# Hybrid decoder layer on one core: sines computed earlier, the picks' transposes placed behind their chunks, new pacing of the gathered rows, low parts in strict turn, a fourth set of split tiles

## The chip, the cores and the metric

The kernel runs on one core of one Trainium2 chip. The metric is the device time of one execution in microseconds (us); of several executions the median is taken. Engines are named as the profile names them: PE (TensorE matmuls), PEld (its weight loads), DVE (VectorE), ACT (ScalarE), POOL (GpSimd) and SP (SyncE, which here issues most of the DMAs).

## The reference

One layer on 512 tokens of width 2048, all in float32:

```python
z = rmsnorm(x) @ w_in                       # columns: pool | q | k | v
x = x + concat(pool_mixer(z), dilated_attention(rope(q), rope(k), v)) @ w_out
x = x + cross_attention(rmsnorm(x), rmsnorm(mem))      # 4 heads, 256 memory tokens
h = rmsnorm(x)
q = (h @ w_pq).reshape(T, 8, 2, 128)
s1, s2 = q[:, :, 0] @ sub_keys_1.T, q[:, :, 1] @ sub_keys_2.T
# per token and head: top 16 of s1 and of s2, their 256 sums, the top 16 of those
gates = softmax(sc); experts = e1 * 128 + e2          # 128 of 16384 experts a token
c = gates * gelu(sum(h * w_u[experts]))
x = x + sum(c * w_v[experts])
out = rmsnorm(x)
```

`rope` turns the first 32 of each head's 128 channels by angles `positions * inv`; it needs sines and cosines of these.

## The kernel before, in words

Every matmul of a weight is split in three, since PE works on rounded operands: a weight tile of 128 x 1024 is loaded by SP (`wraw`), ACT writes its rounded high part `wh` (L143), and DVE or POOL writes the low part `wl = wraw - wh` (L144); `mm3` (L149 to 152) then multiplies `wh` by the high and the low part of the activations, and `wl` by the high part. The pool `wp` holds three pairs `wh`, `wl` and four `wraw`, so the splitting can run about three tiles ahead of PE. A "chunk" is one output block of 128 columns: two such tiles, 48 matmuls (`proj_one`). `lo_eng` says which engine writes the low parts: one for both halves, or a pair for the first and second half.

The 512 tokens are treated in two parts. The first 128 go through the whole attention part alone, in a row layout (0 to 380 us, with `w_pq_f` as the last weight, four groups, 318 to 378 us). Their experts are then evaluated by gathering: for each of 128 picks, POOL issues an indirect DMA that fetches 128 rows of `w_u` (1 MB, L114), DVE takes the dot product with the token (`dot0`, L318); after a gelu the same rows of `w_v` are added up on DVE (`axpy0`, L331). This `queue` of DVE work is threaded between the chunks of everything else: `behind(n)` adds `n` to a debt and issues an entry for each whole unit. The tuple `RATE` sets `n` per chunk by stage: the heads' chunks of `z`, the pool chunks, `w_out`, the cross-attention scores, the scores and picks of `w_pq`, and the gates.

The other 384 tokens follow in the transposed layout: the heads (380 to about 730 us), `w_out` (to 880), cross attention with `w_co` as its last weight (to 991), the scores `w_pq` (to 1137). 64 of them are gathered as well (`dot1`, `axpy1`, their token rows kept in `hy1`); the last 320 go through all 16384 experts densely. The dense part has 128 chunks of `w_u` (`a_chunk`): the first 21 run beside the three `pick`s (7 each, 1137 to 1290), in which DVE finds the top 16 sums of 128 tokens each; 35 more run beside the 80 `gates` (1353 to 1676), in which DVE builds one-hot tiles `u` (L1114, L1116) from the transposed picks and PE multiplies them (L1119). From 1676 us on (`c_chunk`) chunks 56 to 127 are computed and used at once: a group of 8 chunks is multiplied by 16 tiles of `w_v` (the loop over `dd`, PE's L150 to L152 into `pa`), while the next group's 8 chunks of `w_u` are computed (into `pm`). This lasts to 2663 us; the 56 chunks computed before then only need `w_v` (to 3152).

What sets the order: the code's order is handed to a scheduler that works with its own timeline, and it may lay instructions of one engine in another order than the code has; SP and, from the dense part on, POOL keep the code's order. Each engine then runs its list strictly in order. So where a transpose waits for DVE, all matmuls listed behind it wait too.

Three places matter below. In the attention's beginning (L754 to 767) `cosT` and `sinT` are computed from the positions (DVE, with two sines on ACT), and `rope` (L771 to 776) multiplies by them on POOL. In the loop over the picks (L1038 to 1061) PE transposes the pick's result (L1054 to 1056) when DVE has it (`e12`, L1052):

```python
pick(b) ... TE.transpose(pt, e12, ident) x3 ; copies to e12T, gT
a_until(KB * b + KB)      # the 7 chunks of w_u that run beside pick b
```

And in `a_chunk` (L1021 to 1027) the low parts of chunks 64 and up are on POOL for even chunks (both halves) and on DVE for odd ones, while the loop over `dd` has DVE and POOL in turn for `w_v`.

## Time and profile before

| | us |
|---|---|
| median of 3 runs | 3184.94 (3177.57 to 3185.37) |
| the profiled execution's own time | 3175.37 |
| its span | 3173.6 |
| PE busy | 2947.7 (93%) |
| DVE busy | 2422.7 (76%) |
| POOL busy | 1433.8 (45%) |
| ACT busy | 1298.6 (41%) |
| bytes moved | 912.79 MB, mean 288 GB/s |

The busy times are sums over the span; an engine that waits for another is not busy. Since PE leaves 226 us of the span unused, the waits in front of its instructions, stage by stage, are what is to be read. "PEclk" is the granted clock as a share of the full one: a stage with PEclk below 1 has had stretches at half speed, and its busy time is longer by them.

### The profile page before, as it was taken

Reading aid. Unit: us, or ns where it says so; the run is one execution under the profiler, and the core shown is the slowest. Engines: PE = TensorE matmul, PEld = TensorE weight load, DVE = VectorE, ACT = ScalarE, POOL = GpSimd, SP = SyncE. Lnnn points to the kernel's source line nnn. Section 1 sums busy time; section 2 is a strip of 40 time slices with the busy share of each in tenths; the row PEclk is TensorE's granted clock in tenths of the full one; section 3 lists DMA queues with packets and bytes.
Section 4 is the critical chain, followed back from the end, with each engine's and each line's share of the span. In section 5 each row is a group of like instructions: output and inputs, shape, how many; then the busy total and the mean of one; then the engine's idle time right before and its main releaser. Section 6 shows DMA issues by size and latency. Waiting matters only on the chain.

```text
span 3173.6 us, 47405 instructions
## 1 busy us (share of the span) xinstructions
PE 2947.7 (93%) x18311; PEld 2832.5 (89%) x18311; DVE 2422.7 (76%) x3360; ACT 1298.6 (41%) x1789; POOL 1433.8 (45%) x826
## 2 busy tenths in 40 slices
...
GB/s 261 295 300 214 244 119 282 330 309 339 342 266 192 111 127 124 182 302 318 315 304 315 357 325 359 357 367 355 330 372 353 353 354 358 346 357 362 343 163 106
DMA packets 243521, 912.79 MB, mean 288 GB/s; under 512 B 23488, under 2 KB 85600, under 8 KB 192224
## 3 DMA queue, kind: packets, MB, share of 16 engines
...
q8 instruction: 144, 2.36, 0.3%
q14 instruction: 81, 0.66, 0.1%
...
## 4 chain that ended last, share of the span: by engine, by line
PE 66%; DVE 20%; DMA 5%; issue 5%; ACT 2%; POOL 0%; ACTq 0%; POOLq 0%; DVEq 0%; SPq 0%
PE pm L150 11%; PE pm L152 11%; PE pm L151 11%; PE pa L152 9%; PE pa L150 9%; PE pa L151 9%; DVE wl L144 2%; DVE u L1114 2%; DVE oh L295 1%; DVE oh L293 1%; PE pm L400 1%; PE pm L401 1%; PE pm L399 1%; PE pa L1119 1%; DMA rows<-in_w_v_rows_dram,sidx 1%
## 5 line engine op out<-in xcount | busy, mean ns | idle before, releaser
L144 POOL TENSOR_TENSOR wl<-wraw,wh 128x1024 fp32r<-128x1024 f32 x369 | 930.5, 2526 | 1433.3 <-ACT wh L143 1401.4
L143 ACT ACTIVATE wh<-wraw 128x1024 fp32r<-128x1024 f32 (+1 forms) x658 | 693.7, 1058 | 1042.1 <-PE pm L151 467.0
L152 PE MATMUL pa<-ch,wl 128*128 128x320 f32 x2048 | 634.5, 312 | 25.4 <-DVE wl L144 23.5
L150 PE MATMUL pm<-dH,wh 128*128 128x320 f32 x2048 | 640.4, 313 | 15.0 <-DVE cl L1164 6.5
L152 PE MATMUL pm<-dH,wl 128*128 128x320 f32 x2048 | 640.6, 313 | 6.1 <-DVE wl L144 3.9
L150 PE MATMUL pa<-ch,wh 128*128 128x320 f32 x2048 | 636.7, 311 | 7.3 <-DVE xT L1193 4.7
L151 PE MATMUL pm<-dL,wh 128*128 128x320 f32 x2048 | 639.0, 312 | 0.0
L151 PE MATMUL pa<-cl,wh 128*128 128x320 f32 x2048 | 635.3, 310 | 0.0
L144 DVE TENSOR_TENSOR wl<-wraw,wh 128x1024 fp32r<-128x1024 f32 (+1 forms) x289 | 377.4, 1308 | 166.5 <-ACT wh L143 158.7
L152 PEld LDWEIGHTS pa<-ch,wl 128*128 128x128 f32 x2048 | 387.1, 189 | 30.4 <-DVE wl L144 28.1
L150 PEld LDWEIGHTS pm<-dH,wh 128*128 128x128 f32 x2048 | 389.2, 190 | 16.3 <-DVE cl L1164 6.8
L150 PEld LDWEIGHTS pa<-ch,wh 128*128 128x128 f32 x2048 | 388.3, 190 | 10.2 <-ACT ch L1163 5.2
L152 PEld LDWEIGHTS pm<-dH,wl 128*128 128x128 f32 x2048 | 389.3, 190 | 8.2 <-DVE wl L144 5.4
L151 PEld LDWEIGHTS pm<-dL,wh 128*128 128x128 f32 x2048 | 389.3, 190 | 0.0
L151 PEld LDWEIGHTS pa<-cl,wh 128*128 128x128 f32 x2048 | 388.1, 190 | 0.0
L150 PE MATMUL pm<-hH,wh 128*128 128x384 f32 x1024 | 355.9, 348 | 10.4 <-DVE k L811 3.4
L152 PE MATMUL pm<-hH,wl 128*128 128x384 f32 x1024 | 354.2, 347 | 10.5 <-DVE wl L144 10.5
L151 PE MATMUL pm<-hL,wh 128*128 128x384 f32 x1024 | 354.4, 346 | 5.2 <-DVE hL L874 4.4
L1193 DVE TENSOR_TENSOR xT<-pa,xT 128x320 f32<-128x320 f32 x256 | 124.7, 487 | 196.6 <-PE pa L152 191.0
L150 PEld LDWEIGHTS pm<-hH,wh 128*128 128x128 f32 x1024 | 197.6, 193 | 17.1 <-issue 5.8
L152 PEld LDWEIGHTS pm<-hH,wl 128*128 128x128 f32 x1024 | 197.6, 193 | 13.4 <-DVE wl L144 12.5
L151 PEld LDWEIGHTS pm<-hL,wh 128*128 128x128 f32 x1024 | 197.7, 193 | 6.9 <-DVE hL L874 4.7
...
## 6 DMA issues: line engine op xcount, KB each, us to landing
wraw<-in_w_u_dram SPq DMA_DIRECT2D x256, 512.0 KB
wraw<-in_w_v_dram SPq DMA_DIRECT2D x256, 512.0 KB
...
```

The costliest lines, as they stand in the source:

```text
L143: S.activation(wh[:, c], raw[:, c], AF.Copy)
L144: i = (lo_eng or V).tensor_tensor(wl[:, c], raw[:, c], wh.bitcast(F32)[:, c], op=ALU.subtract)
L150: TE.matmul(ps, wh, xh, start=start, stop=False)
L151: TE.matmul(ps, wh, xl, start=False, stop=False)
L152: TE.matmul(ps, wl, xh, start=False, stop=stop)
L293: V.tensor_tensor(oh, iota50.unsqueeze(1).broadcast_to([P, 16, NCAND]), cf[:, h, :].unsqueeze(2).broadcast_to([P, 16, NCAND]), op=ALU.is_e ...
L295: V.tensor_tensor(oh, oh, ecand[:, h, :].unsqueeze(1).broadcast_to([P, 16, NCAND]), op=ALU.mult)
L399: TE.matmul(ps, xh, wh, start=start, stop=False)
L400: TE.matmul(ps, xh, wl, start=False, stop=False)
L401: TE.matmul(ps, xl, wh, start=False, stop=stop)
L1114: V.tensor_tensor(u, iota.unsqueeze(1).unsqueeze(1).broadcast_to([P, 2, 4, P]), e12T[:, :, t:t + 4].unsqueeze(3).broadcast_to([P, 2, 4, P] ...
L1193: V.tensor_tensor(xT[:, dd, NS:], ps[:, :ND], xT[:, dd, NS:], op=ALU.add)
```

## The change

1. **Early sines.** The rope tables are computed in hooks of `w_pq_f`'s third group (`pos_in`, `trig_rows`) instead of at the beginning of the attention; `cosT` lives in the pool `kt`, `sinT` in the first 32 partitions of `accx`.
2. **Picks.** `a_until` stands ahead of the transposes, and the transposes are tied behind the last matmul issued (`issue_after(last_mm)`).
3. **RATE.** (3.0, 2.2, 2.5, 2.0, .25, 1.2) becomes (3.2, 2.4, 2.8, 2.5, .25, .95).
4. **Strict turn.** From chunk 64 on the first half's low part of every `w_u` tile pair is on POOL, the second half's on DVE.
5. **A fourth set of split tiles.** `split_tiles`: once `extra[0]` is set (behind the scores), each fourth load takes its pair `whx`, `wlx` from a new pool `wx`.
6. **Gathered tokens in DRAM.** The 64 tokens' rows are written to `hyd` by ACT's DMA queue in four pieces and loaded by `start1`; `end1` uses a row tile. The pool `hy` is gone.
7. **The sums of squares** in the stage of `w_co` (L961 before) add on POOL instead of DVE.

```diff
-RATE = (3.0, 2.2, 2.5, 2.0, 0.25, 1.2)
+RATE = (3.2, 2.4, 2.8, 2.5, 0.25, 0.95)
...
+    sinT = accx[:32]
...
+    def split_tiles():
+        extra[1] += extra[0]
+        if extra[1] % 4 == 3:
+            return wx.tile([P, 1024], F32R, name="whx"), wx.tile([P, 1024], F32R, name="wlx")
+        return wp.tile([P, 1024], F32R, name="wh"), wp.tile([P, 1024], F32R, name="wl")
...
-        wh = wp.tile([P, 1024], F32R, name="wh")
-        wl = wp.tile([P, 1024], F32R, name="wl")
+        wh, wl = split_tiles()
...
-        TE.matmul(ps, wl, xh, start=False, stop=stop)
+        last_mm[0] = TE.matmul(ps, wl, xh, start=False, stop=stop)
...
-            V.tensor_tensor(acc, acc, q, op=ALU.add)
+            (eng or V).tensor_tensor(acc, acc, q, op=ALU.add)
...
+        def pos_in():
+            posr.append(ep.tile([P, TR], F32, name="jk", bufs=2)[:32].bitcast(I32))
+            nc.scalar.dma_start(posr[0], a["positions"][:, T0:].broadcast_to([32, TR]))
+            nc.scalar.dma_start(invf, a["invfreq"])
+
+        def trig_rows():
+            V.tensor_copy(cosT, posr[0])
+            V.tensor_scalar(cosT, cosT, scalar1=invf, scalar2=None, op0=ALU.mult)
+            trig(cosT, ep.tile([P, TR], F32, name="jk", bufs=2)[:32], sinT, cosT)
+            V.tensor_scalar(sinT[0:16], sinT[0:16], scalar1=-1.0, scalar2=None, op0=ALU.mult)
+
+        hooks_x[2][0] = [pos_in]
+        hooks_x[2][5] = [trig_rows]
...
-        nc.scalar.dma_start(posi, a["positions"][:, T0:].broadcast_to([32, TR]))
-        ang = tmp2k()[:32]
-        V.tensor_copy(ang, posi)
-        V.tensor_scalar(ang, ang, scalar1=invf, scalar2=None, op0=ALU.mult)
-        trig(ang, tmp2k()[:32], sinT, cosT)
...
-                sumsq(xtmp, accx, xT[:, c, :], c == 0, TR)
+                sumsq(xtmp, accx, xT[:, c, :], c == 0, TR, eng=G)
...
-        lo = G if j < RB * KB else (V, G) if j < K1 else G if j < K1 + GRP or j % 2 == 0 else V
+        lo = G if j < RB * KB else (V, G) if j < K1 else G if j < K1 + GRP else (G, V)
...
+            a_until(KB * b + KB)
             pt = pa.tile([P, 512], F32, name="pa")
-            TE.transpose(pt[:, 0:P], e12[:, 0, :], ident)
-            TE.transpose(pt[:, P:2 * P], e12[:, 1, :], ident)
-            TE.transpose(pt[:, 2 * P:3 * P], gtf, ident)
+            with tc.issue_after(last_mm[0].ins):
+                TE.transpose(pt[:, 0:P], e12[:, 0, :], ident)
+                TE.transpose(pt[:, P:2 * P], e12[:, 1, :], ident)
+                TE.transpose(pt[:, 2 * P:3 * P], gtf, ident)
...
-            a_until(KB * b + KB)
...
-        S.copy(gx[0], hy1)
+        r = row_tile()
+        nc.sync.dma_start(r, hyd)
+        S.copy(gx[0], r)
...
-        y1[0] = hy.tile([P, D], F32, name="htok")
+        y1[0] = row_tile()
...
-            S.copy(hy1[:, k4 * 512:(k4 + 1) * 512], pt)
+            hs4 = gw.tile([P, 512], F32, name="hs4")
+            S.copy(hs4, pt)
+            nc.scalar.dma_start(hyd[:, k4 * 512:(k4 + 1) * 512], hs4)
```

How this moves instructions is seen in the engines' lists. Line numbers in a list of the changed kernel are its own: its `rope` is L790 to 792, its transposes of a pick L1073 to 1075, its low part L153, its `mm3` L161 to 163, its dot products of the second queue L1095.

POOL, the beginning of its list up to the first head's rope, before (`t2k` is the shuffled copy of `q` or `k`):

```order
L144 TENSOR_TENSOR wl_3339<-wraw_3337,wh_3338 128x1024
L144 TENSOR_TENSOR wl_3441<-wraw_3439,wh_3440 128x1024
L144 TENSOR_TENSOR wl_3579<-wraw_3577,wh_3578 128x1024
L774 TENSOR_TENSOR t2k_3224<-t2k_3224,sinT_3203 32x384
L774 TENSOR_TENSOR t2k_3239<-t2k_3239,sinT_3203 32x384
L775 TENSOR_TENSOR q_3222<-q_3222,cosT_3202 32x384
L775 TENSOR_TENSOR k_3235<-k_3235,cosT_3202 32x384
L776 TENSOR_TENSOR q_3222<-q_3222,t2k_3224 32x384
L776 TENSOR_TENSOR k_3235<-k_3235,t2k_3239 32x384
```

and now:

```order
L153 TENSOR_TENSOR wl_3337<-wraw_3335,wh_3336 128x1024
L153 TENSOR_TENSOR wl_3439<-wraw_3437,wh_3438 128x1024
L790 TENSOR_TENSOR t2k_3222<-t2k_3222,accx_93 32x384
L791 TENSOR_TENSOR q_3220<-q_3220,cosT_116 32x384
L790 TENSOR_TENSOR t2k_3237<-t2k_3237,accx_93 32x384
L791 TENSOR_TENSOR k_3235<-k_3235,cosT_116 32x384
L792 TENSOR_TENSOR q_3220<-q_3220,t2k_3222 32x384
L792 TENSOR_TENSOR k_3235<-k_3235,t2k_3237 32x384
```

Two low parts stand ahead of the rope instead of three, and the sine (`accx`) and cosine tiles come from the stage before.

PE, the second pick's transposes, before:

```order
L152 MATMUL pm_10381<-dH_7905,wl_10414 128x320
L150 MATMUL pm_10445<-dH_7905,wh_10447 128x320
L151 MATMUL pm_10445<-dL_7906,wh_10447 128x320
L1054 MATMUL pa_10117<-ident_86,e12_10111 128x128
L1055 MATMUL pa_10117<-ident_86,e12_10111 128x128
L1056 MATMUL pa_10117<-ident_86,gt_10103 128x128
L152 MATMUL pm_10445<-dH_7905,wl_10448 128x320
```

and now:

```order
L162 MATMUL pm_10531<-dL_7933,wh_10563 128x320
L163 MATMUL pm_10531<-dH_7932,wl_10564 128x320
L1073 MATMUL pa_10595<-ident_86,e12_10136 128x128
L1074 MATMUL pa_10595<-ident_86,e12_10136 128x128
L1075 MATMUL pa_10595<-ident_86,gt_10128 128x128
L161 MATMUL pm_10707<-dH_7932,wh_10709 128x320
L162 MATMUL pm_10707<-dL_7933,wh_10709 128x320
```

They stood in the middle of a chunk and now stand behind one. Counted from the first matmul of `dH`, pick 0's come behind 387 of them (379 before), pick 1's behind 641 (547), pick 2's behind 977 (730); the first gate's matmul behind 1221 (1134).

DVE, a piece of the stage with `w_u` and `w_v`, before (L1075 is a dot product, L1159 and L1164 make `ch`, `cl` of a chunk, L1193 adds a `w_v` product):

```order
L1075 ISA rows,sact_7900<-rows,gx 128x2048
L1075 ISA sact_7900 128x1
L144 TENSOR_TENSOR wl<-wraw,wh 128x1024
L1075 ISA rows,sact_7900<-rows,gx 128x2048
L1075 ISA sact_7900 128x1
L144 TENSOR_TENSOR wl<-wraw,wh 128x1024
L1159 TENSOR_TENSOR pm<-pm,gt 128x320
L1193 TENSOR_TENSOR xT<-pa,xT 128x320
L144 TENSOR_TENSOR wl<-wraw,wh 128x1024
```

and now:

```order
L153 TENSOR_TENSOR wlx<-wraw,whx 128x1024
L1095 ISA rows,sact_7927<-rows,gx 128x2048
L1095 ISA sact_7927 128x1
L153 TENSOR_TENSOR wl<-wraw,wh 128x1024
L1181 TENSOR_TENSOR pm<-pm,gt 128x320
L1186 TENSOR_TENSOR cl<-pm,ch 128x320
L153 TENSOR_TENSOR wlx<-wraw,whx 128x1024
```

Before, DVE's low parts belonged to loads that followed one another (the run over the engines was DVE, three times POOL, three times DVE, POOL); now each is every second load, and each second of these goes to the fourth set.

## Rows read from the trace of the kernel before

**Rows 1.** The page's head: the span, and section 1's busy times

```profile
span 3173.6 us, 47405 instructions
PE 2947.7 (93%) x18311; PEld 2832.5 (89%) x18311; DVE 2422.7 (76%) x3360; ACT 1298.6 (41%) x1789; POOL 1433.8 (45%) x826
```

**Rows 2.** Windows: stretch, length, busy of the engines (instructions), PEclk, DMA share, GB/s

```profile
318.00:378.00 60.00, 50.72 (x232) 38.10 (x231) 51.62 (x127) 34.76 (x39) 1.30 (x1) 0.99 0.79 263
398.00:428.00 30.00, 11.20 (x36) 9.02 (x35) 29.97 (x119) 7.14 (x14) 6.12 (x6) 0.60 0.12 36
480.00:960.00 480.00, 444.77 (x2378) 420.17 (x2377) 385.82 (x478) 184.57 (x319) 244.09 (x171) 0.96 0.83 310
1137.00:1290.00 153.00, 121.52 (x775) 119.03 (x774) 147.92 (x377) 50.63 (x65) 88.56 (x34) 0.89 0.42 130
1353.00:1676.00 323.00, 304.45 (x2166) 299.91 (x2165) 304.08 (x249) 161.31 (x177) 154.80 (x70) 0.98 0.84 307
1741.00:2663.00 922.00, 912.81 (x6184) 910.97 (x6183) 666.39 (x634) 327.38 (x398) 493.83 (x298) 0.99 0.92 352
2663.00:3040.00 377.00, 350.97 (x2311) 344.41 (x2310) 296.21 (x306) 122.36 (x148) 182.64 (x107) 0.98 0.92 343
```

**Rows 3.** Timeline of PE at the attention's start: start, length, line, [idle before <-releaser]

```profile
411.68 1.22 PE L818 MATMUL pa<-kT,q 128*128 128x128 f32 x4 [13.33 <-POOL q L776]
...
416.34 0.80 PE L818 MATMUL pa<-kT,q 128*128 128x128 f32 x2 [2.06 <-DVE t2k L822]
...
421.82 0.66 PE L150 MATMUL pm<-hH,wh 128*128 128x384 f32 x1 [3.40 <-DVE k L811]
```

**Rows 4.** Timeline of PE: the picks' transposes

```profile
1212.44 0.48 PE L1054 MATMUL pa<-ident,e 128*128 128x128 f32 x1 [1.80 <-DVE e L1052]
...
1252.09 0.47 PE L1054 MATMUL pa<-ident,e 128*128 128x128 f32 x1 [10.96 <-DVE e L1052]
...
1289.66 0.45 PE L1054 MATMUL pa<-ident,e 128*128 128x128 f32 x1 [8.03 <-DVE e L1052]
```

**Rows 5.** PE's waits: in 1290:1741 (first row), 1741:2663 (two), 2663:3040 (last)

```profile
PE pa L1119 <- DVE u L1116: 14.7, 11, 3.6
...
PE pa L152 <- DVE wl L144: 6.7, 3, 3.0
PE pm L152 <- DVE wl L144: 2.5, 4, 0.7
...
PE pa L152 <- DVE wl L144: 16.8, 14, 2.3
```

**Rows 6.** Timelines of ACT, DVE and POOL before the attention's start

```profile
395.10 1.28 ACT L236 ACT_TABLE_LOAD   x1
401.23 0.52 ACT L236 ACTIVATE sinT<-t2k 32x384 f32<-32x384 f32 x1 [4.85 <-DVE t2k L235]
...
386.00 0.55 DVE L811 TENSOR_TENSOR k<-ma,r2c 128x384 f32<-128x384 f32 x1
...
386.82 2.39 POOL L144 TENSOR_TENSOR wl<-wraw,wh 128x1024 fp32r<-128x1024 f32 x1 [7.77 <-ACT wh L143]
...
403.88 2.28 POOL L774 TENSOR_TENSOR t2k<-t2k,sinT 32x384 f32<-32x384 f32 x2 [6.34 <-DVE sinT L767]
408.74 0.98 POOL L775 TENSOR_TENSOR q<-q,cosT 32x384 f32<-32x384 f32 x1 [2.57 <-DVE cosT L239]
```

**Rows 7.** Groups by line: DVE over the span; in 940:991; POOL over the span

```profile
L318 DVE CUSTOM_DVE_ANT_0 rows<-rows,gx 128x2048 f32<-128x2048 f32 x66 | 150.0, 2276 | 6.4 <-DMA rows<-in_w_u_rows_dram,sidx 6.4
...
L217 DVE SCALAR_TENSOR_TENSOR hL<-xT,gains,hH 128x384 fp32r<-128x384 f32 x16 | 19.4, 1219 | 4.1 <-ACT hH L216 4.1
...
L225 DVE TENSOR_TENSOR accx<-accx,xtmp 128x384 f32<-128x384 f32 x15 | 8.2, 546 | 0.0
...
L1219 POOL TENSOR_TENSOR xT<-xT,rf 128x384 f32<-128x384 f32 x5 | 6.4, 1315 | 15.1 <-ACT rf L210 15.1
```

**Rows 8.** Timelines of DVE and POOL near 2800 us

```profile
2796.93 0.48 DVE L1159 TENSOR_TENSOR pm<-ga,gt 128x320 f32<-128x320 f32 x1
...
2799.56 2.23 DVE L1159 TENSOR_TENSOR pm<-ga,gt 128x320 f32<-128x320 f32 x1
...
2799.04 2.39 POOL L144 TENSOR_TENSOR wl<-wraw,wh 128x1024 fp32r<-128x1024 f32 x1 [4.79 <-ACT wh L143]
```

More of the change, by code (lines that the diff above doesn't have):

```diff
@@ L94, in hybrid_kernel @@
     rz = const.tile([P, NB], F32, name="rz")[:, :RB]
+    invf = const.tile([32, 1], F32, name="invf")
     accx = const.tile([P, TR], F32, name="accx")
+    sinT = accx[:32]
     xT = big.tile([P, KD, TR], F32, name="xT")
@@ L133, in hybrid_kernel @@
     anchor = [None]
+    extra = [False, 0]
+    def split_tiles():
[3 more added lines that the diff above has]
+        return wp.tile([P, 1024], F32R, name="wh"), wp.tile([P, 1024], F32R, name="wl")
     def load_w(src, lo_eng=None, parts=1):
         raw = wp.tile([P, 1024], F32, name="wraw", bufs=WRAW)
-        wh = wp.tile([P, 1024], F32R, name="wh")
-        wl = wp.tile([P, 1024], F32R, name="wl")
+        wh, wl = split_tiles()
         n = 1024 // parts
@@ L147, in load_w @@
         return wh, wl
+    last_mm = [None]
     def mm3(ps, wh, wl, xh, xl, start, stop):
@@ L365, in hybrid_kernel @@
     halo = kt.tile([P, 8, 16], F32, name="halo")
+    cosT = kt.tile([32, TR], F32, name="cosT")
     def alloc_ma():
@@ L711, in hybrid_kernel @@
             hooks_x[k // 8][k % 8] = [lambda k=k: xr_sq(k)]
+        posr = []
+        def pos_in():
[9 more added lines that the diff above has]
+        hooks_x[2][5] = [trig_rows]
         for g in range(4):
```

11 lines of the change are left out of this document (3 added, 8 removed).

## The prediction

> **What bounds the kernel now.** First the page's head [rows 1]: PE is busy for 2947.7 of 3173.6 us. What can be won without changing PE's work is the other 226 us, and what PE loses to a lower clock while it is busy. No other engine is near the span as a whole (DVE 76%), but a mean hides stages, so the second view is a table of windows, one per stage [rows 2]. There the reader sees three kinds of stage. In 1741 to 2663 PE is busy for 912.81 of 922 us at a granted clock of 0.99, so 9.2 us are all that waits can give. In 2663 to 3040 it is busy for 350.97 of 377, while DMA is at 0.92. And from 1137 to 1290 and from 1353 to 1676 DVE is busy for 147.92 of 153 and for 304.08 of 323 us: there DVE is about as much the bound as PE. The third view is the timeline and the waits, which say what PE stood for. At the attention's start it waits 13.33 us for POOL's rope, then 2.06 and 3.40 us [rows 3]; at the picks' transposes 1.80, 10.96 and 8.03 us [rows 4]; in the gates 14.7 us for the one-hot tiles, and in the dense part for late low parts on DVE [rows 5].
>
> One figure for the pace: 6184 matmuls of 128 x 320 took 912.81 us in 1741 to 2663, 0.1476 us each [rows 2].
>
> **The change, part by part.**
>
> *Early sines: -12 us.* The 13.33 us end with the last rope instruction on POOL. Going back [rows 6]: POOL began at 403.88, after the sine on ACT (401.23), which waited 4.85 us for the angles on DVE; then POOL waited another 2.57 us for the cosine. With the tables there, what is left is `k` (386.00, done at 386.55), two shuffles on DVE, POOL's low part until 389.21 (one of the three is now behind the rope) and the rope: two products in 2.28 us and four instructions of 0.98, together 6.2. That ends at 395.4, 3 us before PE's last chunk (411.68 - 13.33 = 398.35). So the 13.33 go; the next to wait for are the scores' masks and the next chunk on DVE, the 2.06 and 3.40 us that stand there now, in a stretch where DVE is busy for 29.97 of 30 us. I let them grow by 1.3. Ends: -6 if POOL's list is held up by its low parts, -17 if the clock (0.60 in 398 to 428, [rows 2]) recovers as well.
>
> *The price of it: +2.* Two extra loads of ACT's tables, 1.28 us each [rows 6], and eleven DVE instructions go into the first part, whose last stage has DVE busy for 51.62 of 60 us; in the list only three of the eleven fall there, the others in the stage of `w_cq`. The positions' DMA is issued long before. Ends 0 and +4.
>
> *RATE: +4 before the scores, -5 in the gates.* A dot product takes 2.276 us of DVE [rows 7]. By the stages' chunk counts the heads take 2.2 more, the pool chunks 1.6, `w_out` 4.8, the cross scores 2: 10.6, or 24 us of DVE and 11 MB, between 480 and 960, where DVE has 94 us free, and DMA at 0.83 has 82 [rows 2]. In the gates 35 x 0.25 = 8.75 fewer, -20 us of DVE in 323, where PE waits 14.7 us for `u`. Of that I count a third, since DVE remains at 284 of 304 needed by PE. Ends 0 and +15 before, -12 and +10 in the gates.
>
> *Sums of squares on POOL: -3.* Fifteen additions of 0.546 us leave DVE, 8.2 us of a 51-us stage. Nearest price on POOL: 1.315 for a product of the same shape, 20 us in all [rows 7]. What speaks against it: DVE's instruction with two inputs in SBUF runs long beside POOL: 2.23 us beside a low part that POOL began at 2799.04, against 0.48 alone [rows 8]; the `hL` of this stage average 1.219 us. More POOL work makes more such meetings; at 20 more us of it, eight instructions of DVE held for half an addition each are 5 us. The Trainium skill ("SBUF — State Buffer", Who interferes with whom) says the same: a DVE instruction with two inputs in SBUF contends with a GpSimd instruction that reads SBUF, and the later one blocks until the other is done. By that rule alone this edit would give back its 8 us; the trace's 2.23 against 0.48 agrees with it. Ends -6 and +5.
>
> *Picks: -27.* PE's list says what is moved: pick 1's transposes 94 matmuls later, pick 2's 247. At 0.1476 that is 13.9 and 36.5 us, against waits of 10.96 and 8.03 [rows 4]. DVE's picks take as long as now (147.92 of 153). PE came to pick 1's at 1252.09 - 10.96 = 1241.1; it will come at 1255, 3 us behind DVE. To pick 2's it came at 1281.6, of which 11 are then gone: 1270.6 + 36.5 = 1307, 17 behind DVE. So both waits go, and 1 of pick 0's 1.80: 20. The clock's dips that follow such waits go too: 775 matmuls at 0.1476 are 114.4 against the 121.52 shown, 7 us. What is late next: the gates. Their first matmul now comes 87 matmuls (12.8 us) later in PE's list, which leaves DVE nearly as much time as before. Ends -32, and -12 if pick 1's stays.
>
> *Strict turn and a fourth set: -8 in 1741 to 2663, -10 in 2663 to 3040.* In the first stretch PE waits 6.7 + 2.5 us for low parts [rows 5]; with the splitting one load further ahead (24 matmuls, 3.5 us) a low part that is 3.0 late at most comes in time. No more than these 9.2 and a little clock is there. In the second PE loses 26 us, 16.8 of them for DVE's low parts, 14 times, at most 2.3. By the same measure all would go, but DMA is busy for 0.92 of 377 = 347 us there: no less time than PE's own 351. I take 10, ends 0 and -25; for the first stretch +5 and -17.
>
> *Tokens in DRAM: 0.* Four copies and DMAs of 256 KB on ACT and one load of 1 MB on SP, among a thousand loads; its cover is the four `wraw` tiles loaded ahead (14 us). Without that cover it costs the 3 us of one MB at 350 GB/s.
>
> Sum: -12 + 2 + 4 - 5 - 3 - 27 - 8 - 10 = -59, against the profiled execution's 3175.37: 3116. That execution is 9.6 us under the median of the runs and 2 below their lowest, so a median of runs should be some us higher; I add 5: **3121 us**.
>
> **The rivals.**
>
> 1. *DMA holds the dense part.* Then strict turn and the fourth set give nothing: 3121 + 18 = **3139 us**. For it: 0.92 busy at 352 and 343 GB/s [rows 2]. Against it: low parts, not loads, are what PE waited for [rows 5]. The Trainium skill ("SBUF — State Buffer", Summary) gives about 358 GB/s as the limit for traffic between HBM and SBUF; the trace's means lie within 5% of it.
>
> 2. *The earlier dots cost their time.* The 24 us of DVE in 480 to 960 come on PE's path instead of 4: **3141 us**. For it: DVE is busy for 386 of 480 us, in bursts around the picks and softmaxes. Against: 94 us are free.
>
> 3. *The moves don't move the waits.* DVE reaches pick 1 and 2 later, or the rope still waits (for POOL's low parts), so that sines and picks give nothing: 3121 + 39 = **3160 us**. For it: 3 us of margin at pick 1. Against: 17 at pick 2.
>
> 4. *Slower: the strict turn lays POOL's low part beside each of DVE's.* DVE's, with two inputs in SBUF, is then held for the rest of POOL's 2.4 us, and comes late as often as it is held. Its price is that of the late ones today, 16.8 / 14 = 1.2 us, and as much again where the clock falls behind it: 2.4. From (59 - 18 + 10) / 2.4 = 21 late ones on the kernel is slower; with 35 of the 120 DVE low parts in the first stretch late it takes 3139 + 84 = **3223 us**. For it: 2.23 against 0.48 [rows 8]. Against: POOL's share of the loads is the same half as before, and DVE has 256 us free there.
>
> **How the numbers follow.** Forecast 0.50; rivals 1 to 4: 0.16, 0.10, 0.07, 0.07; 0.10 for the gains' upper ends, about 3090. A measurement can tell 0.3% from no change, 9.6 us: faster is below 3175.4, slower above 3194.5. Rival 4 is slower, half of rival 3's bounds reach no change, and some of the others' upper ends do: 0.86, 0.07, 0.07. The sum of all lower ends is 3066 and of all upper ones 3196; neither comes at once. The range 3086 to 3166 holds the forecast and rivals 1 to 3, and leaves out rival 4 and what lies under 3086.
>
> **What would show it.** Early sines: the wait of 13.33 for `q` L776 is gone, those behind it stay under 8 us. Picks: no transpose waits over 2 us, PEclk in that stage 0.95 or more. RATE: DVE about 410 of 480 us in 480 to 960, PE's waits for `u` under 12. Dense part: waits for `wl` under 3 us in the first stretch, under 8 in the second, with PE busy for over 0.95 of it. Wrong would be: new waits in front of the gates as large as those removed; more waits for `wl`; a transfer or POOL as the releaser in 480 to 990.

## The result, and the profile after

The change makes the kernel slower. Four runs of each, side by side: 3211.67 us (3209.63 to 3220.22) against 3181.26 us (3176.87 to 3185.37) before; the ratio of the two means is 1.0101, 95% interval 1.0075 to 1.0127. The prediction said 3121, in a range of 3086 to 3166.

The page of the changed kernel, its head:

```profile
span 3207.8 us, 47207 instructions
PE 2949.9 (92%) x18311; PEld 2829.1 (88%) x18311; DVE 2467.5 (77%) x3345; ACT 1289.1 (40%) x1790; POOL 1501.6 (47%) x841
```

Beside [rows 1]: PE has the same 18311 matmuls and 2.2 us more of busy time, so the other 32 of the 34 us by which the span is longer are waits; DVE is busy for 45 us more although it lost 15 additions. The windows, with stretches that hold about the same work as those of [rows 2]:

```profile
398.00:428.00 30.00, 21.66 (x110) 19.51 (x109) 30.00 (x111) 11.66 (x20) 11.76 (x5) 0.83 0.21 58
480.00:960.00 480.00, 427.00 (x2309) 401.34 (x2308) 400.03 (x485) 179.97 (x307) 256.42 (x182) 0.96 0.86 329
1145.00:1300.00 155.00, 131.27 (x836) 129.97 (x835) 148.83 (x375) 54.61 (x71) 101.99 (x37) 0.91 0.45 135
1737.00:2672.00 935.00, 912.46 (x6118) 905.25 (x6117) 700.36 (x619) 313.42 (x390) 502.16 (x289) 0.99 0.90 340
2677.00:3065.00 388.00, 348.71 (x2298) 341.70 (x2297) 308.96 (x306) 117.89 (x144) 191.28 (x109) 0.97 0.92 343
```

In 398 to 428 PE now does 110 matmuls where it did 36: the sines work. In 480 to 960 it does 2309 instead of 2378, with DVE busier. In the stage with `w_u` and `w_v` it does 6118 in 935 us where it did 6184 in 922, and DVE is busy for 34 us more.

The clearest reading is to follow PE through its own list: both kernels have the same matmuls in each stage, so the time at which the first or the n-th of a kind starts is a mark. A kind is named by the activations that it multiplies (`hH` and its low part `hL` counted together, likewise `dH`, `dL`) or by its weight. The difference of each stage's length, after minus before, beside what the prediction's terms said:

| stage, ended by (us before) | predicted | measured |
|---|---|---|
| A: the first 128 tokens, last matmul of `w_pq_f` (372.0) | +2 | +2.6 |
| B: the attention's start, 519th matmul of the `mm3` lines by `hH`, `hL` (431.6) | -12 | -14.4 |
| C: heads, pool chunks, `w_out`, 2420th by `hH`, `hL` (851.1) | +4 (C and D) | +12.5 |
| D: cross attention, `w_co`, scores, first by `dH` (1136.8) | -3 | +7.2 |
| E: picks, 922nd by `dH`, `dL` (1315.6) | -27 | -9.3 |
| F: gates and the first eight chunks, first of `w_v` (1740.9) | -5 | -2.7 |
| G: `w_u` and `w_v`, 3073rd of `w_v` (2657.3) | -8 | +23.4 |
| H: `w_v` alone, the last of `w_v` (3151.0) | -10 | +15.1 |

B came as forecast. C, D, G and H lose 58 us where 17 were to be gained, and E gains a third of what it should. Between the -59 of the forecast and the 34 measured lie 93 us: 56 in G and H, 19 in C and D, 18 in E. The marks carry noise. A is the same code in all the kernels below but b2 and is 2.4 to 8.1 us longer than in the profile before; in b2, which changes nothing there, it is 3.7 longer. So A's +2.6 shows no price of the sines. Two kernels that differ in E alone (f2 and p1) are 13 us apart in H.

PE's waits, in 630:730, 860:1010, 1145:1300 and 1737:2672 of the changed kernel:

```profile
PE pm L161 <- DVE q L866: 10.0, 3, 4.1
PE pa L881 <- issue: 7.7, 1, 7.7
...
PE pm L161 <- DVE xT L975: 15.1, 8, 3.7
PE pm L163 <- DVE wl L153: 9.8, 1, 9.8
...
PE pa L1073 <- DVE e L1069: 15.6, 2, 10.7
PE pm L161 <- ACT ga L1043: 8.1, 2, 5.6
...
PE pa L163 <- DVE wl L153: 17.9, 6, 3.4
PE pm L163 <- DVE wlx L153: 4.4, 13, 1.0
```

All but two name DVE, and of these L881 waits for `k`, which DVE ended 0.1 us before (shown below). In the pool chunks PE waits for their chain on DVE (`q`, L866, and `k`); in `w_co` for the sums `xT`; in the picks for DVE still, in two places instead of three; in the dense part six times for a low part of `w_v`, where the kernel before waited three times [rows 5].

### The profile page after: what moved, and what is told of

The parts are those of the page before. It is cut to its first block, busy times and chain, and to the rows that moved or that the text cites. A ratio compares the mean times of both kernels' runs of the same rounds, so it can differ in the third digit from the quotient of the medians.

```text
span 3207.8 us, 47207 instructions
## 1 busy us (share of the span) xinstructions
PE 2949.9 (92%) x18311; PEld 2829.1 (88%) x18311; DVE 2467.5 (77%) x3345; ACT 1289.1 (40%) x1790; POOL 1501.6 (47%) x841
## 4 chain that ended last, share of the span: by engine, by line
PE 66%; DVE 20%; DMA 5%; issue 5%; ACT 2%; POOL 1%; ACTq 1%; DVEq 0%; SPq 0%; POOLq 0%
PE pm L163 11%; PE pm L161 11%; PE pm L162 11%; PE pa L163 9%; PE pa L161 8%; PE pa L162 8%; DVE wlx L153 2%; PE pa L1141 2%; DVE wl L153 1%; PE pm L412 1%; PE pm L413 1%; PE pm L411 1%; DVE rows L329 1%; DVE oh L304 1%; DVE oh L306 1%
## 5 line engine op out<-in xcount | busy, mean ns | idle before, releaser
L153 POOL TENSOR_TENSOR wl<-wraw,wh 128x1024 fp32r<-128x1024 f32 x355 | 887.0, 2500 | 1408.1 <-ACT wh L152 1361.6
L152 ACT ACTIVATE wh<-wraw 128x1024 fp32r<-128x1024 f32 (+1 forms) x530 | 557.4, 1057 | 697.6 <-PE pm L162 315.0
L161 PE MATMUL pa<-ch,wh 128*128 128x320 f32 x1792 | 560.5, 313 | 16.3 <-DVE xT L1215 13.2
L161 PE MATMUL pm<-dH,wh 128*128 128x320 f32 x1280 | 403.0, 315 | 11.2 <-ACT ga L1043 8.1
L163 PE MATMUL pm<-dH,wl 128*128 128x320 f32 x1280 | 402.4, 314 | 0.0
L162 PE MATMUL pm<-dL,wh 128*128 128x320 f32 x1280 | 402.2, 314 | 0.1
L161 PE MATMUL pm<-hH,wh 128*128 128x384 f32 x1024 | 355.6, 347 | 21.4 <-DVE q L866 10.0
L161 PEld LDWEIGHTS pa<-ch,wh 128*128 128x128 f32 x1792 | 342.6, 191 | 18.3 <-issue 14.2
L153 DVE TENSOR_TENSOR wl<-wraw,wh 128x1024 fp32r<-128x1024 f32 (+1 forms) x175 | 244.4, 1398 | 61.1 <-ACT wh L152 59.8
L161 PEld LDWEIGHTS pm<-dH,wh 128*128 128x128 f32 x1280 | 245.3, 192 | 12.0 <-ACT ga L1043 8.6
L162 PEld LDWEIGHTS pm<-dL,wh 128*128 128x128 f32 x1280 | 245.4, 192 | 0.4 <-DVE dL L228 0.4
L163 PE MATMUL pm<-dH,wlx 128*128 128x320 f32 x768 | 241.2, 314 | 4.6 <-DVE wlx L153 4.4
L163 PEld LDWEIGHTS pm<-dH,wl 128*128 128x128 f32 x1280 | 245.0, 191 | 0.3 <-POOL wl L153 0.3
L161 PE MATMUL pm<-dH,whx 128*128 128x320 f32 x768 | 238.7, 311 | 0.0
L162 PE MATMUL pm<-dL,whx 128*128 128x320 f32 x768 | 238.3, 310 | 0.0
```

The costliest lines, as they stand in the source:

```text
L152: S.activation(wh[:, c], raw[:, c], AF.Copy)
L153: i = (lo_eng or V).tensor_tensor(wl[:, c], raw[:, c], wh.bitcast(F32)[:, c], op=ALU.subtract)
L161: TE.matmul(ps, wh, xh, start=start, stop=False)
L162: TE.matmul(ps, wh, xl, start=False, stop=False)
L163: last_mm[0] = TE.matmul(ps, wl, xh, start=False, stop=stop)
```

## The experiments

Eighteen kernels, each timed beside the kernel before. "Ratio" is the time against that; the eight columns are each stage's length minus that of the kernel before, in us. They come from one profiled execution of each kernel, which can lie well off its median (e4's is 16 us above it, v3's 12). Two ratios that are less than about 0.003 apart are not told apart by their intervals.

| run | ratio, 95% interval | A | B | C | D | E | F | G | H |
|---|---|---|---|---|---|---|---|---|---|
| the change | 1.0101, 1.0075 to 1.0127 | 2.6 | -14.4 | 12.5 | 7.2 | -9.3 | -2.7 | 23.4 | 15.1 |
| e1_rate | 1.0089, 1.0067 to 1.0111 | 4.4 | -14.3 | -2.5 | 0.5 | -6.1 | -5.3 | 27.9 | 18.5 |
| e2_turn | 1.0014, 0.9997 to 1.0031 | 8.1 | -14.1 | 9.9 | 6.9 | -9.1 | -11.2 | -0.2 | 12.7 |
| e3_three_sets | 1.0128, 1.0091 to 1.0166 | 4.6 | -14.5 | 8.9 | 6.2 | -7.1 | -5.3 | 27.9 | 13.5 |
| e4_acc_dve | 1.0054, 1.0033 to 1.0075 | 5.2 | -12.8 | 16.3 | -0.1 | -10.3 | -3.6 | 19.0 | 21.6 |
| f1_rate_turn | 0.9961, 0.9939 to 0.9982 | 3.3 | -14.4 | -1.8 | -0.5 | -9.8 | -6.3 | -5.6 | 26.7 |
| f2_rate_turn_acc | 0.9937, 0.9913 to 0.9960 | 5.3 | -13.8 | -2.3 | -6.5 | -6.4 | -3.4 | -5.3 | 20.5 |
| f3_sines_picks | 0.9990, 0.9976 to 1.0004 | 4.6 | -13.6 | -2.0 | -6.4 | -6.8 | 5.2 | 11.1 | 15.9 |
| p1_picks_old | 0.9937, 0.9916 to 0.9958 | 4.9 | -12.6 | -4.3 | -7.1 | 0.7 | -3.6 | -7.3 | 7.2 |
| d1_no_gather | 0.9821, 0.9783 to 0.9860 | 6.1 | -14.5 | -3.1 | -9.0 | -10.3 | -0.5 | -5.2 | -21.4 |
| g1_pool_halves | 1.0052, 1.0033 to 1.0070 | 2.5 | -14.2 | 9.3 | 5.6 | -12.7 | -9.8 | 17.0 | 8.9 |
| h1_halves | 0.9884, 0.9854 to 0.9914 | 2.4 | -13.7 | -3.3 | -7.0 | -14.8 | -10.4 | 1.0 | 6.6 |
| h2_halves_grp | 0.9893, 0.9862 to 0.9924 | 4.9 | -13.9 | -1.9 | -6.1 | -13.2 | -10.3 | 9.0 | -2.0 |
| t1_turn_halves | 0.9979, 0.9962 to 0.9996 | 5.3 | -14.0 | -2.9 | -8.6 | -13.2 | -0.1 | 16.1 | 15.2 |
| q1_quarters | 0.9922, 0.9897 to 0.9947 | 7.2 | -13.9 | -2.3 | -7.2 | -16.7 | -12.1 | 13.4 | 13.4 |
| b1_before_sines | 0.9957, 0.9935 to 0.9979 | 4.7 | -14.5 | -2.6 | -8.1 | 2.3 | 5.7 | -4.3 | 5.1 |
| b2_before_halves | 0.9926, 0.9903 to 0.9949 | 3.7 | 0.6 | -0.2 | -2.4 | -3.9 | -10.2 | -15.3 | 5.2 |
| v3_gv_swap | 1.0063, 1.0043 to 1.0084 | 5.2 | -14.0 | 17.2 | 8.1 | -6.4 | -2.2 | 24.0 | 7.2 |
| v4_pairs_best | 0.9921, 0.9903 to 0.9939 | 4.1 | -14.1 | -3.2 | -8.5 | -13.3 | -0.2 | 17.7 | -6.3 |

### One part undone at a time

```diff
e1_rate:        RATE = (3.0, 2.2, 2.5, 2.0, 0.25, 1.2)
e2_turn:        - lo = ... G if j < K1 + GRP else (G, V)
                + lo = ... G if j < K1 + GRP or j % 2 == 0 else V
e3_three_sets:  - extra[0] = True
e4_acc_dve:     - sumsq(xtmp, accx, xT[:, c, :], c == 0, TR, eng=G)
                + sumsq(xtmp, accx, xT[:, c, :], c == 0, TR)
```

**e1_rate.** 

> The change with RATE as before. Theory A (the earlier dot products stand in front of the pool chunks', w_out's and w_co's chains on DVE): from 640 to 1000 us PE's lead over the kernel before falls by some 24 us, and this gives it back; the first matmul of dH comes near 1124 us instead of 1145 and the time is about 3190 us. Rival: the stalls there come from the new places of the sines and of the sums of squares; then the lead at dH stays and the time stays within 5 us of the changed kernel's 3212.

Theory A held in its place and size: C and D together go from +19.7 to -2.0 us, the first matmul of `dH` comes at 1125.0. The time did not follow clearly: the ratio falls by 0.0012, inside the intervals, and G and H, still with the strict turn, lose 46 us. What the dots do in the pool chunks is plain in the changed kernel's timelines of DVE and, in the last row, of PE:

```profile
639.29 2.26 DVE L872 TENSOR_TENSOR t2k<-q 128x399 f32<-128x399 f32 x1
641.47 2.27 DVE L329 CUSTOM_DVE_ANT_0 rows<-rows,gx 128x2048 f32<-128x2048 f32 x1
...
643.75 0.54 DVE L876 SCALAR_TENSOR_TENSOR k<-t2k,q 128x384 f32<-128x384 f32 x1
644.21 1.21 DVE L153 TENSOR_TENSOR wl<-wraw,wh 128x1024 fp32r<-128x1024 f32 x1
645.35 0.55 DVE L866 TENSOR_TENSOR q<-pm,r2c 128x384 f32<-128x384 f32 x1
...
713.45 2.27 DVE L329 CUSTOM_DVE_ANT_0 rows<-rows,gx 128x2048 f32<-128x2048 f32 x1
...
716.14 2.27 DVE L329 CUSTOM_DVE_ANT_0 x<-x,gx 128x2048 f32<-128x2048 f32 x1
...
720.14 0.56 DVE L876 SCALAR_TENSOR_TENSOR k<-t2k,q 128x384 f32<-128x384 f32 x1
...
720.80 1.62 PE L881 MATMUL pa<-k,pts 128*128 128x384 f32 x2 [7.66 <-issue]
```

A dot of 2.27 us stands between two steps of a chunk's chain; PE waits 4.1 us for the `q` at the end, which frees its accumulator (`pm`). Near 720 two dots stand in front of `k`, and PE waits 7.66 us. In e1 PE waits 3.8 us for `q` instead of 10.0, and not at L881.

**e2_turn.** 

> The change without the strict turn (even chunks of w_u on POOL, odd on DVE, from chunk 64 on). Theory B (the turn puts a POOL low part beside each DVE one of w_v, which is then held and late): the six waits of about 3 us between 2369 and 2647 go, the stage from 1737 to 2672 gets some 20 us shorter, and the time is about 3190 us. Rival C (the fourth set does it): no change there, 3205 to 3215.

Theory B's place held: G goes from +23.4 to -0.2, the time by 0.87% (28 us). PE's waits in 1735:2648 of this run are two instead of six:

```profile
PE pa L163 <- DVE wl L153: 10.9, 2, 5.4
```

**e3_three_sets.** 

> The change with three sets of split tiles as before, the turn kept. Rival C (the fourth set lets loads run ahead until DMA issues on ACT's queue stand at the switch to the groups without w_u, and lists high parts behind a chunk's gelu): the waits of 3 us and the one of 11 us near 2703 go, and the time is about 3175 us. Theory B (the turn does it): the waits of 3 us stay, at most the one of 11 goes: 3200 to 3212.

Rival C fell: with three sets and the turn G is +27.9 and the ratio 1.0128. Undoing the fourth set does not help, so the turn is what costs.

**e4_acc_dve.** 

> The change with the sums of squares of the w_co stage on DVE as before. If POOL's additions hold DVE's two-input instructions there (seven waits of PE for xT, 15 us together, where before there were five of 8 us): 5 us less, about 3207 us. If they cost nothing: within 3 us of 3212.

D falls from +7.2 to -0.1, as expected or a little more, and the time by 0.47%, more than D explains; the profiled execution, from which D is read, is no shorter than the changed kernel's (C and H are longer in it by 4 and 6 us). The additions in the changed kernel's 940:1008, on POOL:

```profile
L236 POOL TENSOR_TENSOR accx<-accx,xtmp 128x384 f32<-128x384 f32 x15 | 16.9, 1124 | 6.8 <-ACT xtmp L235 6.5
```

An addition costs 1.124 us on POOL (0.546 on DVE, [rows 7]). What PE loses by it is shown at f2, which differs from f1 in this alone.

### Several parts undone, and POOL's instruction cut in two

```diff
f1_rate_turn:      e1_rate and e2_turn together
f2_rate_turn_acc:  e1_rate, e2_turn and e4_acc_dve together
f3_sines_picks:    f2 and e3_three_sets
g1_pool_halves (on the change; extra[0] is set behind the scores):
+            if lo_eng is G and extra[0]:
+                for hc in (slice(0, 512), slice(512, 1024)):
+                    i = G.tensor_tensor(wl[:, hc], raw[:, hc], wh.bitcast(F32)[:, hc], op=ALU.subtract)
... else the one instruction as before
```

**f1_rate_turn.** 

> The change with both RATE and the turn as before. If the two causes are apart and add up: the first w_v matmul near 1718 us as with RATE alone undone (1741 before), the stage after it as with the turn alone undone, some 10 us lost at the switch to the groups without w_u: ratio to the kernel before 0.993 to 0.998. If the dense part eats any lead that it is given (a bound by DMA, or the debt of gathered rows that comes with the old RATE): 1.000 to 1.005.

0.9961, as expected. With the turn undone, RATE is worth 0.53% (e2 to f1), not the 0.12% that it was worth beside the turn.

**f2_rate_turn_acc.** 

> The same with the sums of squares on DVE as well. If POOL's additions cost anything beside the old RATE: 2 to 5 us less than the run with RATE and turn undone; if not, within 2 us of it.

0.24% less, some 8 us, which the two intervals alone would not tell from nothing; D falls by 6.0, and by 7.3 in the pair with the new RATE (e4). DVE's group `hL` in 926:988 and the end of the stage in f1, then the same of f2 (its group in 925:985):

```profile
L228 DVE SCALAR_TENSOR_TENSOR hL<-xT,gains,hH 128x384 fp32r<-128x384 f32 x16 | 23.6, 1482 | 6.7 <-ACT hH L227 6.7
...
980.02 2.28 DVE L329 CUSTOM_DVE_ANT_0 x<-x,gx 128x2048 f32<-128x2048 f32 x1
...
982.23 0.15 DVE L197 TENSOR_SCALAR rw<-pa 128x3 f32<-128x3 f32 x1
...
982.44 0.69 PE L161 MATMUL pa<-hH,wh 128*128 128x384 f32 x1 [4.94 <-DVE rw L197]
```

```profile
L228 DVE SCALAR_TENSOR_TENSOR hL<-xT,gains,hH 128x384 fp32r<-128x384 f32 x16 | 19.4, 1217 | 4.0 <-ACT hH L227 4.0
...
973.58 0.16 DVE L197 TENSOR_SCALAR rw<-pa 128x3 f32<-128x3 f32 x1 [0.98 <-PE pa L209]
```

With the sums on POOL, DVE has begun a dot when PE has added up the last sum (its L209, near 974), and `rw`, which reads that result, stands behind four dots; PE waits 4.94 us for it. With the sums on DVE, `rw` comes first and PE doesn't wait. The changed kernel, e1 and e2 have the same wait (4.4 to 5.1 us); e4 has 0.3. The longer `hL` are 4.2 us of DVE, but PE's waits for `xT` hardly differ (9.1 in f1, 8.0 in f2).

**f3_sines_picks.** 

> The same with three sets of split tiles: what is left of the change is the early sines, the picks' transposes and the tokens in DRAM. If the fourth set is worth anything with the old turn (the prediction's theory of loads one tile further ahead): slower than the last run by 5 to 15 us, all in 1741 to 3040. If the fourth set is worth nothing: within 3 us.

0.53% slower than f2, 17 us; G is 16.4 us longer and F 8.6, H 4.6 shorter. With the old turn the fourth set is worth more here than the 8 us that the prediction gave to both parts in G; beside the strict turn (e3) it was worth 0.27%, within the intervals. It was tried only beside the tokens in DRAM: the kernel before with the sines alone (b1, three sets) is slower than f2 by 0.20%, within the intervals, and its G is as short. So part of what the fourth set gains may be what the tokens cost.

**g1_pool_halves.** 

> The whole change, but each low part that POOL writes in the dense part is two instructions of 512 columns instead of one of 1024. If DVE's late low parts are held by POOL's whole instruction (2.9 us against 1.2 alone, 1.7 of the 2.9 us of each of the six waits), a hold ends after 1.2 us at most: the waits fall to about 1.7 us and the time by 10 to 20 us, to a ratio near 1.005. If they are late because of their place in DVE's list alone, the waits stay and the ratio is 1.010 to 1.013.

The ratio falls to 1.0052, as if the hold (DVE's instruction with two inputs standing until POOL's ends, [rows 8]) were the cause. But later runs say otherwise of the turn (t1, b2).

### What the picks, the gathers and the halves are worth

```diff
h1_halves:      f2 with g1's two instructions
h2_halves_grp:  h1, and in the first group's eight chunks  - behind(RATE[5])  + behind(0.3)
d1_no_gather:   f2, and in axpy1
-    r = row_tile()
-    rows(r, a["w_v_rows"], sidx2[:, k:k + 1])
+    r = spare[0]
p1_picks_old:   f2, a_until and the three transposes as in the kernel before
```

**h1_halves.** 

> RATE, the turn and the sums of squares as before (as in f2_rate_turn_acc), and POOL's low parts in the dense part in two instructions of 512 columns. If POOL's whole instructions also hold DVE with the old turn (there 30 of 129 low parts on DVE were held, 58 us together, though few were late): the ratio falls from 0.994 to 0.988 to 0.992. If what is late there is set by DMA: 0.992 to 0.996.

0.9884: the fastest kernel of the study that computes everything, 1.2% under the kernel before, a span of 3133.9 us. Against f2 the picks (E) get 8.4 us shorter and F 7.0; G is not shorter in these profiles.

**h2_halves_grp.** 

> The same, and the eight chunks of the first dense group carry 0.3 instead of 1.2 gathered rows each (the rest goes later). If the wait of 17 us before the sixth of these chunks comes from DVE standing at its list's head for a gathered row (9.3 us) with the chunk's product behind it, it falls to about 3 us as in the changed kernel and the time by some 14 us, to 0.985 to 0.988; if the chunk waits for the gates' table from DRAM, the wait stays.

0.9893, no gain, and F stays: PE waits 16.3 us for `cl` in the first eight chunks, 16.6 in h1. The gathered rows were not what these chunks lose. With the new RATE the wait is short (3.2 us in the changed kernel, 4.0 in e2); why was not followed further.

**d1_no_gather.** 

> As f2_rate_turn_acc, but the 64 gathers of w_v rows of the second queue are left out (DVE's 64 additions read a tile that is there already), so that in the groups without w_u half the bytes are gone, DVE's work stays. If DMA sets the pace there (0.87 to 0.98 busy, 518 us from the first matmul of the ninth group to the last, where PE alone would need 454): 465 to 480 us. If late low parts on DVE set it: over 500 us.

This kernel leaves out the gathers and adds a tile that is there already; it was run twice. H is 472.3 us, the only run with a clear gain there (the others, v4 and h2, have 6 and 2 us). The windows 2625:2996 of f2 (first row) and of this run:

```profile
2625.00:2996.00 371.00, 332.27 (x2149) 325.57 (x2149) 289.63 (x290) 111.82 (x138) 181.98 (x103) 0.96 0.91 336
```

```profile
2625.00:2996.00 371.00, 360.90 (x2427) 355.87 (x2427) 291.88 (x323) 129.12 (x158) 121.40 (x50) 1.00 0.62 189
```

2427 matmuls instead of 2149 in the same time, with DMA busy for 0.62 instead of 0.91 and DVE just as busy. So gathers, with their bytes and POOL's time for issuing them, set the pace in H, not DVE's work. Both were taken away together, so which of the two it is stays open.

**p1_picks_old.** 

> As f2_rate_turn_acc, but the picks' transposes where they were before. If the move is worth what the prediction said (27 us): a ratio near 1.002. If DVE sets the picks' end (the wait moved to pick 0, 13.8 us, and to pick 1, 5.4 us, with the move): 5 to 10 us slower than with the move, 0.995 to 0.997.

The ratio is f2's to the fourth digit: neither expectation came. PE's waits for the picks' transposes without the move:

```profile
1195.17 0.48 PE L1071 MATMUL pa<-ident,e 128*128 128x128 f32 x1 [10.64 <-DVE e L1069]
...
1233.71 0.47 PE L1071 MATMUL pa<-ident,e 128*128 128x128 f32 x1 [10.82 <-DVE e L1069]
...
1273.00 0.45 PE L1071 MATMUL pa<-ident,e 128*128 128x128 f32 x1 [9.66 <-DVE e L1069]
```

and with it (f2):

```profile
1200.44 0.48 PE L1073 MATMUL pa<-ident,e 128*128 128x128 f32 x1 [13.78 <-DVE e L1069]
...
1245.10 0.48 PE L1073 MATMUL pa<-ident,e 128*128 128x128 f32 x1 [5.44 <-DVE e L1069]
...
1267.30 0.63 PE L161 MATMUL pm<-dH,wh 128*128 128x320 f32 x1 [6.26 <-ACT ga L1043]
```

31.1 us of waits become 25.5, with a new one for ACT. E is 7.1 us shorter with the move, and the difference is no longer seen in the median.

### What the strict turn costs by

```diff
t1_turn_halves:    h1 with (G, V) from chunk 64 on
q1_quarters:       h1 with four instructions of 256 columns
b1_before_sines:   the kernel before with part 1 of the change alone
b2_before_halves:  the kernel before with g1's two instructions
v3_gv_swap:        the change, and for w_v  - lo_eng=G if dd % 2 else V  + lo_eng=V if dd % 2 else G
v4_pairs_best:     v3 with RATE and the sums as before, and two instructions
```

**t1_turn_halves.** 

> As h1_halves, but with the strict turn. If the turn costs by POOL's hold alone, little of its 28 us is left when the hold is at most 1.2 us: a ratio of 0.987 to 0.992. If the turn puts low parts late in DVE's list as well: 0.993 to 0.998.

0.9979 against h1's 0.9884: 0.95%, as much as with whole instructions (e2: 0.87%). DVE's low parts in G still take 1.66 us on the mean here, so this run did not take the holds away; but together with e2 and e3 (below) it says that the hold is not what the turn costs by. Theory B was right on the part and wrong on the mechanism.

**q1_quarters.** 

> As h1_halves, with POOL's low parts in four instructions of 256 columns. If what is left of the hold (1.2 us) still costs: 0.983 to 0.987. If POOL's extra instructions cost as much as the shorter holds bring: 0.987 to 0.993.

0.9922, slower than halves, at the upper end of the second expectation; E gains 1.9 more, G loses 12.4. In G POOL is busy for 575 us instead of 529, DVE for 658 instead of 688, and PE still waits for low parts on DVE (14.1 us, six times). So the shorter holds bring nothing there; that POOL's added work is what costs was expected, and is not shown.

**b1_before_sines.** 

> The kernel before with the early sines alone. By the prediction's term, minus 12 plus 2: 0.996 to 0.998. If the dense part's last stretch takes a lead back as it does in the other runs: 0.998 to 1.001, with PE 10 to 14 us ahead up to 2650 us.

0.9957, some 14 us: the term was right, and the lead arrives at the end. On the way D is 8.1 us shorter, though nothing there was edited (PE waits 8.1 us for `xs` in the cross attention of the kernel before, 0.9 here), and E and F are 8.0 longer.

**b2_before_halves.** 

> The kernel before with POOL's low parts, from the picks on, in two instructions. If the hold costs the kernel before too (13 of its 130 low parts on DVE were held in the stage with w_u and w_v, and DVE is the bound in the picks): 0.992 to 0.997, half of it in the picks. If it is a cost of the strict turn and the fourth set only: 0.998 to 1.002.

0.9926, some 23 us, on the kernel before with nothing else: 14 in E and F, 15 in G, where in this run's profile PE has no wait at all that the view lists. That fits a hold that costs the kernel before, in the picks above all, but the low parts show it only in part: DVE's in G take 4.5 us less in all. Low parts in G, DVE's in the kernel before and here, and POOL's halves:

```profile
L144 DVE TENSOR_TENSOR wl<-wraw,wh 128x1024 fp32r<-128x1024 f32 x128 | 170.1, 1332 | 99.1 <-ACT wh L143 91.9 <-issue 6.8
```

```profile
L150 DVE TENSOR_TENSOR wl<-wraw,wh 128x1024 fp32r<-128x1024 f32 x128 | 165.6, 1295 | 146.4 <-ACT wh L144 146.3
...
L148 POOL TENSOR_TENSOR wl<-wraw,wh 128x512 fp32r<-128x512 f32 x257 | 330.9, 1315 | 309.7 <-ACT wh L144 302.1 <-PE pa L157 5.5 <-PE pa L158 1.4
```

**v3_gv_swap.** 

> The whole change, but w_v's low parts have their engines swapped (POOL for even tiles, DVE for odd ones), so that the loads go POOL, POOL, DVE, DVE instead of strictly in turn; the shares stay. In ACT's list 50 of 55 gelus of this stage then stand behind two high parts more than the least, against 9 of 55 in the changed kernel. If the place of the high parts behind the gelu is what the turn costs: ACT's wait before the gelu falls from 6.0 to under 3 us, the six waits of 3 us go, and the ratio falls from 1.010 to 0.998 to 1.003. If POOL's holds or the alternation in itself cost it: 1.006 to 1.012.

The place of ACT's high parts fell as well, or is only a part: ACT's wait before the gelu did fall, from the changed kernel's (first row; 371.7 / 62 = 6.0 us) to 3.2 (the groups of ACT in 1741:2650 of each):

```profile
L1043 ACT ACTIVATE pm<-pm 128x320 f32<-128x320 f32 x62 | 26.2, 422 | 371.7 <-PE pm L163 371.7
```

```profile
L1043 ACT ACTIVATE pm<-pm 128x320 f32<-128x320 f32 x63 | 26.6, 422 | 202.0 <-PE pm L163 202.0
```

but G stays at +24.0, with PE waiting for the chunks' second halves on DVE instead (29.2 us in 31 waits). The ratio, 1.0063, lies at the lower end of the second expectation.

**v4_pairs_best.** 

> The same order of loads in pairs, with RATE and the sums of squares as before and POOL's low parts in two instructions (h1_halves with pairs in place of the old turn). If the place in ACT's list decides: as fast as h1_halves or faster, 0.984 to 0.989. If the old turn is better for another reason: 0.990 to 0.996.

0.9921: the old turn (h1) is better by 0.4%. H is the shortest of all complete kernels (-6.3), G loses 17.7. Against t1, from which it differs by the order of `w_v`'s engines alone, it is 0.58% faster, with G as long and H 21.5 us shorter; between v3 and the changed kernel, the same pair with whole instructions, it is 0.38%. So part of what the strict turn costs lies in H and goes with the order of `w_v`; H's own 13 us of noise leave open how much.

## Why the prediction was wrong

**Early sines, -12 and +2: right.** B -14.4, alone 0.9957; the +2 is within the noise of A. The rope ended on POOL at 398.1 instead of 395.4, since a low part ran until 391.2; the wait for the masks grew to 6.63 us (the prediction: 2.06 and 3.40, grown by 1.3), and still the 13.33 went.

**RATE, "+4 before the scores, ... +15": the step that failed first.** Undoing it is worth 21.7 us in C and D, over the upper bound, and 0.53% of the time where the turn is undone too. The mechanism was rival 2's, at nearly its price of 24. The step took "where DVE has 94 us free" as cover. Free time is of use only where it lies: the scheduler laid the dots of 2.27 us into the chains of the pool chunks, whose results PE waits for next (10.0 us for `q` and 7.66 for `k`, against 3.8 and none in e1). PE's wait of 9.8 us for a low part near 877, in `w_out`, is not theirs: e1 has it with the old RATE, 9.85 us at 864.01. The -5 in the gates did not come either. PE waits 15.4 us for `u` in the changed kernel, 14.7 before, and 5.3 in e1; what e1 loses instead is one wait of 18.4 us for `cl` in the first dense chunks, 3.2 in the changed kernel.

**Sums of squares on POOL, -3: wrong sign.** It costs some 6 us in D (f1 to f2), 8 by the ratios. "8.2 us of a 51-us stage" leave DVE, but the path ends elsewhere: `rw`, behind the last sum, now stands after four dots, and PE waits 4.94 us for it, a wait that the term did not have. The rule set beside the edit there (the Trainium skill, "SBUF — State Buffer", Who interferes with whom) says that DVE's two-input instruction and POOL's reading one exclude each other. `hL`'s mean of 1.482 us in f1 against 1.217 in f2 agrees, but that is the smaller part of what PE loses.

**Picks, -27: mis-sized by its premise.** E gained 9.3 us. The transposes moved as listed, but the premise "DVE's picks take as long as now" with a free PE in front did not hold. PE came to the first pick's transposes 66.5 us after the first matmul of `dH` (73.8 before, having lost more on the way), and the pick was ready after 77.2 (75.6):

```profile
1221.95 0.47 PE L1073 MATMUL pa<-ident,e 128*128 128x128 f32 x1 [10.65 <-DVE e L1069]
...
1266.85 0.48 PE L1073 MATMUL pa<-ident,e 128*128 128x128 f32 x1 [4.90 <-DVE e L1069]
```

From the first to the second pick DVE needed 44.9 us (39.7 before, [rows 4]), PE's chunks in between only 254 x 0.1476 = 37.5. In a stage in which DVE is busy for 148 of 155 us the waits go where PE next needs DVE. One came back through ACT, for `ga` (5.59 us before a chunk at 1289): ACT's copy of the second pick's gates, in front of the gelu that frees PE's accumulator, waited for DVE's copy of the same transposes, which came 15 us after them:

```profile
1283.45 0.27 ACT L1079 COPY gT<-pa 128x128 f32<-128x128 f32 x1 [20.18 <-DVE e12T L1078]
```

With POOL's low parts in halves E is 3.4 to 8.4 us shorter in three pairs (the change and g1, before and b2, f2 and h1), so part of DVE's time there is holds by POOL.

**Strict turn and fourth set, -8 in the first stretch: the larger miss.** The two were costed as one, by the loads running one tile further ahead. The fourth set, with the old turn, is worth 16.4 us there (f3 to f2, beside the tokens in DRAM). The turn costs 15 to 34 us of G in the three pairs that differ by it alone (t1 and h1 15.1, the change and e2 23.6, e1 and f1 33.5). Rival 4 named this part as the slower side and gave it 0.07. DVE's low parts did take longer in the changed kernel, as it said (first two rows), but they do so without the turn as well (e2, the next two, in 1741:2672) and hardly with the turn and three sets (e3, the last, in 1741:2672):

```profile
L153 DVE TENSOR_TENSOR wlx<-wraw,whx 128x1024 fp32r<-128x1024 f32 x63 | 121.2, 1923 | 4.8 <-ACT whx L152 4.8
L153 DVE TENSOR_TENSOR wl<-wraw,wh 128x1024 fp32r<-128x1024 f32 x64 | 99.5, 1554 | 17.8 <-ACT wh L152 16.5 <-issue 1.2
```

```profile
L153 DVE TENSOR_TENSOR wl<-wraw,wh 128x1024 fp32r<-128x1024 f32 x96 | 159.1, 1661 | 42.3 <-ACT wh L152 42.0
...
L153 DVE TENSOR_TENSOR wlx<-wraw,whx 128x1024 fp32r<-128x1024 f32 x34 | 50.9, 1497 | 24.5 <-ACT whx L152 24.5
```

```profile
L153 DVE TENSOR_TENSOR wl<-wraw,wh 128x1024 fp32r<-128x1024 f32 x126 | 178.3, 1416 | 40.0 <-ACT wh L152 40.0
```

The mean is 1.332 us before, 1.74 in the changed kernel, 1.62 in e2 and 1.42 in e3. So the longer low parts come with the fourth set; e2 has them and loses nothing in G, e3 nearly lacks them and loses 27.9 us. The hold, rival 4's mechanism, is therefore not what the turn costs by, and that its 3223 us came near the 3212 measured is luck. In t1 halving POOL's instruction does not give the turn's cost back, and v3 shows that the place of ACT's high parts does not either. What the versions with the longest G have in common (the change, e1, e3, e4, g1, t1, v3, v4: 16 us and more) is that DVE writes the second half of every chunk, where before it wrote both halves of every second one. Why that is late is open.

**The stretch with `w_v` alone, -10: did not come.** H is longer by 5 to 27 us in every complete run but h2 and v4. The step that failed is that a load split further ahead takes the low parts' waits away: PE waits 19.5 us for them in 2677 to 3065 of the changed kernel (16.8 before, [rows 5]). Rival 1's bound holds here: without the gathers H is 21 us shorter than before (d1). It is no ceiling of the traffic as such: 2300 to 2400 of the kernel before moved 380 GB/s, this stretch 343. Why most changed versions take longer there than the kernel before, with the same bytes, isn't settled; in the changed kernel one part is a stop of ACT at the switch, where issuing a 160 KB load took 10.16 us, DVE's next low part waited for ACT, and PE for DVE:

```profile
2688.20 10.16 ACTq L1179 DMA_DIRECT2D ga<-gad  x1
2698.41 2.00 ACT L152 ACTIVATE wh<-wraw 128x1024 fp32r<-128x1024 f32 x2 [13.24 <-issue]
...
2699.50 1.23 DVE L153 TENSOR_TENSOR wl<-wraw,wh 128x1024 fp32r<-128x1024 f32 x1 [11.01 <-ACT wh L152]
...
2703.53 0.60 PE L161 MATMUL pa<-ch,wh 128*128 128x320 f32 x1 [11.13 <-DVE xT L1215]
```

**Tokens in DRAM, 0:** not tried alone. Sines, picks' move and tokens together (f3, three sets) are 0.33% slower than the sines alone (b1); the picks' move made no difference to the time in the one pair that has it alone (f2 and p1, four sets), so something of that may lie here, and this is not shown.
